# Turning a residual sum and an input into channels: VectorE's 32x32 blocks read back from DRAM in place of TensorE's transposes

## The chip, the core and the metric

The kernel runs on one NeuronCore of a Trainium2 chip. Its engines are TensorE (PE in the profile, its weight loads PEld), VectorE (DVE), ScalarE (ACT), GpSimd (POOL) and SyncE (SP). DMAs are issued by an engine's instruction stream: here by SP (queue q1) and by ACT (queue q10). The metric is the device time of one execution in microseconds (us); lower is better.

## The reference

One layer of a decoder trunk over 512 tokens of 2048 channels, in float32, and a final RMSNorm. The part that matters here is its end:

```python
x = x + einsum('btc,cd->btd', y_mix, w_out)          # 512x2048 @ 2048x2048: the residual sum, "x2" below
gate = sigmoid(einsum('btd,de->bte', x, w_pg) + b_pg)  # 512x2048 @ 2048x2048
x = x + gate * einsum('btq,qd->btd', p, w_ple)       # p is 512x256, w_ple 256x2048
return rms_norm(x, final_g)
```

Everything ahead of it (the input projections, a recurrence over 16 heads, a pooling group) produces `y_mix`.

## The kernel before, in words

**Tiles.** T = 512 tokens are NT = 4 tiles of P = 128; D = 2048 channels are KT = 16 steps of 128; an output block is EC = 512 channels, so that there are four, `ec` = 0 to 3. TensorE contracts over partitions, so a left operand has to lie channels by tokens. All large products are made of three float32r products of a high and a low part (`mm3`: hi·hi, hi·lo, lo·hi); `split` and `wsplit` make the two parts, the high one by a cast on ACT, the low one by a subtraction on DVE.

**The projections (`proj`).** For an output block, `proj` walks 16 weight steps. A step loads 256 KB of weights on SP (`raw_o`, `raw_g`: four buffers), splits it into `whi` and `wlo` (four buffers each; cast on ACT, subtraction on DVE) and issues 12 matmuls: 4 token tiles by 3 products. So a load may be issued only when DVE has made the low part of the step four back, and a cast only when TensorE has finished the step four back. A tile name such as `raw_g0_7` is the block (0) and the weight step (7).

**The out-projection** (`acc_o`, blocks 0 to 3) comes first. After each block DVE adds x (`x2_..`, line 1026) and ACT's queue stores the sum to DRAM as `x2d` (line 1027), 128 rows by 512 channels at a time. `turn` then makes channels out of tokens: 16 TensorE transposes of 128x128 into PSUM (`px2_..`, line 1033; the profile calls the tile `px`), and a `split` of each of the four 128x512 results into `x2hi` and `x2lo`, which are what the gate products (`acc_g`) contract. For blocks 0 to 2 `turn` runs while the next block's matmuls go on; for block 3 it is called from inside the first gate block, behind its third step (`aside`), and followed by the loads of the first embedding rows (`recall(0, lp)`, tiles `pler`). The gate block reads the channels of x2's block 3 only from its weight step 12 on.

**The gate stage.** Three blocks and then a last one with an order of its own. Each block reads its x2 rows again from DRAM (`fetch`, tiles `x2r`, line 1134), the embedding product (`pler`) and two rows of parameters (`bB`, `gB`), all on ACT's queue.

**The input p.** Before the out-projection, while the last head pair's recurrence runs, ACT's queue loads p (`pn`, line 927), TensorE transposes it (8 transposes, tile `ppt`, line 161) and two splits give `phi` and `plo` for the embedding product (`pple`). The recurrence has a chain of its own through SP: `xw` is written to DRAM (`xd`), read back as `x1` (tile `x` in the profile, line 689) and turned by DVE (`y1`, line 732) before TensorE's small products can start.

**The order.** Up to the out-projection TensorE's order is that of the program (`pin`). Behind it a scheduler places instructions on each engine; each engine then runs its own list in order and waits where it must. A DMA reports on one of eight completion semaphores in turn, shared by the two queues, and a DMA that is given one of them waits until that semaphore's previous DMA has landed.

Of the kernel before, what the change touches and what calls it, by code (L numbers as in the profile page):

```python
# [9 lines left out]
F32 = mybir.dt.float32  # L10
# [5 lines left out]
P = 128  # L16
T = 512
D = 2048
KT = D // P
NT = T // P  # L20
# [5 lines left out]
DPLE = 256  # L26
# [8 lines left out]
def trunk_kernel(ctx: ExitStack, tc: tile.TileContext, x, p, norm_g, w_in, mu, w0, w_up, a0, a_up,  # L35
                 k_k, k_a, r_k, ln_w, ln_b, w_pool, pool_scale, w_out, w_ple, w_pg, b_pg, final_g, out):
    nc = tc.nc
    PSUM = bass.MemoryType.PSUM
    x, p, w_in, w_out, w_ple, w_pg = x[0], p[0, 0], w_in[0], w_out[0], w_ple[0], w_pg[0]
    out = out[0]  # L40

    cst = ctx.enter_context(tc.tile_pool(name="cst", bufs=1))
    dram = ctx.enter_context(tc.tile_pool(name="dram", bufs=2, space=bass.MemoryType.DRAM))
# [4 lines left out]
    psM = s2.enter_context(tc.tile_pool(name="psM", bufs=3, space=PSUM))  # L48
# [45 lines left out]
    for h in range(2):  # L94
        rows = slice(64 * h, 64 * h + 64)
# [40 lines left out]
    def split(hi, lo, src):  # L136
        c_ = nc.scalar.copy(hi, src)
        nc.vector.tensor_tensor(lo, src, hi.bitcast(F32), ALU.subtract)
        return c_
# [20 lines left out]
    def tr(*a):  # L160
        i = nc.tensor.transpose(*a)
        return tc.keep_in_program_order(i) if pin[0] else i

    def mm3(ps, wh, wl, xh, xl, first, last):
        mm(ps, wh, xh, start=first, stop=False)
        mm(ps, wh, xl, start=False, stop=False)
        return mm(ps, wl, xh, start=False, stop=last)
# [293 lines left out]
    def stream():  # L461
        for kind, nm, j in jobs:
            if kind == "b":
                yield from pool_unit(j)
                continue
            if kind == "e":
                yield from embed_unit(j)
                continue
            if kind == "p":
                for k in range(2):  # L470
                    pt = psM.tile([P, T], F32, name=f"ppt{k}", tag="m")
                    for tt in range(NT):
                        tr(pt[:, tt * P:(tt + 1) * P], pn[0][:, tt, k * P:(k + 1) * P], ident)
                    a_ = rw.tile([P, T], F32R, name=f"phi{k}", tag=("sk", "sr")[k], bufs=2)
                    b_ = rw.tile([P, T], F32R, name=f"plo{k}", tag=("sv", "sg")[k], bufs=2)
                    split(a_, b_, pt)
                    phl.append((a_, b_))
                yield 3
                continue
            ps = psA.tile([P, T], F32, name=f"z{nm}{j}", tag="acc")  # L480
            yield from zcols(ps, f"{nm}{j}")
            t_ = rw.tile([P, T], F32, name=f"s{nm}{j}", tag=f"s{nm}", bufs=2)
            if nm == "g":
                silu2(ps, t_)
            else:
                shifted(ps, t_, {"r": 0, "k": 8, "v": 16}[nm] + j)
            zt[nm, j] = t_
# [429 lines left out]
    for j in range(NJ):  # L917
        def between():
            pump(H3 if j + 1 < NJ else HC[2])
            if j + 1 < NJ:  # L920
                scores(j + 1)
                pump_to(H2)

        if j + 1 == NJ:
            pn.append(rw.tile([P, NT, DPLE], F32, name="pn", tag="ar", bufs=2))
            for h in range(2):
                nc.scalar.dma_start(out=pn[0][:, 2 * h:2 * h + 2, :],
                                    in_=p[256 * h:256 * h + 256, :].rearrange("(t p) q -> p t q", p=P))
        if j + 1 < NJ:
            prepare(j + 1)  # L930
        elif gates:
            gates.pop()()
        recur(j, invert(j + 1) if j + 1 < NJ else iter(()), between)
        if j + 1 < NJ:
            gather(j + 1)
# [21 lines left out]

    x2hi = hp.tile([P, KT, T], F32R, name="x2hi", tag="ahi")
    x2lo = hp.tile([P, KT, T], F32R, name="x2lo", tag="alo")
    x2d = dram.tile([T, D], F32, name="x2d", bufs=1)  # L960

    KEEP, LATE = 8, 4
    TP = 40
# [4 lines left out]
        pool, tag = (psB, "accb") if nacc[0] % 5 in (1, 2, 3) else (psA, "acc")  # L968
        return pool.tile([P, EC], F32, name=nm, tag=tag)

    def proj(w, hi_, lo_, ec, nm, ks=range(KT), tts=range(NT), keep=None, aside=None):
        acc = {tt: acc_tile(f"acc_{nm}{ec}_{tt}") for tt in tts}
        for i, k in enumerate(ks):
            src = w[k * P:(k + 1) * P, ec * EC:(ec + 1) * EC].unsqueeze(1)
            if nm == "o" and ec == 0 and i + AHEAD < KT:
                load_y(ks[i + AHEAD])
            if (f"{nm}{ec}_{k}", 0) in ready:
                wh, wl = ready.pop((f"{nm}{ec}_{k}", 0))
            elif nm == "o" and ec == 0 and i < 4:
                wh, wl = chunk(f"{nm}{ec}_{k}", 0)  # L980
            elif keep is None or LATE <= i < KT - KEEP:
                wh, wl = wsplit(src, 1, EC, f"{nm}{ec}_{k}")
            else:
                raw = wp.tile([P, 1, EC], F32, name=f"raw_{nm}{ec}_{k}", tag="raw")
                nc.sync.dma_start(out=raw, in_=src)
                if i < 2:
                    if i == 0:
                        two = [pp.tile([P, 2, EC], F32R, name=f"{g}k", tag=g, bufs=1) for g in ("dh", "dl")]
                    wh, wl = (g[:, i:i + 1, :] for g in two)
                else:  # L990
                    own = i < KT - 4
                    wh, wl = ((kp_ if own else wp).tile([P, 1, EC], F32R, name=f"{g}k{k}",
                                                        tag=f"{g}k{k}" if own else g) for g in ("whi", "wlo"))
                split(wh, wl, raw)
                keep[k] = (wh, wl)
                if i >= LATE:
                    continue
            for tt in tts if keep is None or i >= LATE else tts[:-1]:
                ts_ = slice(tt * P, (tt + 1) * P)
                first = i == (LATE if keep is not None and tt == NT - 1 else 0)  # L1000
                e_ = mm3(acc[tt], hi_[:, k, ts_], lo_[:, k, ts_], wh[:, 0, :], wl[:, 0, :], first, i == KT - 1)
            if aside is not None and i == 2:
                with tc.issue_after(e_.ins):
                    hi = aside()
                with tc.issue_after(hi.ins):
                    recall(0, lp)
        return acc

    ples = {}
# [1 line left out]
    def recall(ec, pool):  # L1011
        ples[ec] = []
        for tt in range(NT):
            t_ = pool.tile([P, EC], F32, name=f"pler{ec}_{tt}", tag="ple", bufs=4)
            nc.scalar.dma_start(out=t_, in_=pled[tt * P:(tt + 1) * P, ec * EC:(ec + 1) * EC])
            ples[ec].append(t_)

    for ec in range(D // EC):
        es = slice(ec * EC, (ec + 1) * EC)
        acc = proj(w_out, yhi, ylo, ec, "o", order)  # L1020
        x2 = []
        for tt in range(NT):
            rows = slice(tt * P, (tt + 1) * P)
            t_ = pp.tile([P, EC], F32, name=f"x2_{ec}_{tt}", tag=("u", "sw")[tt // 2])
            nc.scalar.dma_start(out=t_, in_=x[rows, es])
            nc.vector.tensor_tensor(t_, acc[tt], t_, ALU.add)
            nc.scalar.dma_start(out=x2d[rows, es], in_=t_)
            x2.append(t_)
        def turn(ec=ec, x2=x2):
            for i in range(EC // P):  # L1030
                pt = psM.tile([P, T], F32, name=f"px2_{ec}_{i}", tag="m")
                for tt in range(NT):
                    nc.tensor.transpose(pt[:, tt * P:(tt + 1) * P], x2[tt][:, i * P:(i + 1) * P], ident)
                hi = split(x2hi[:, 4 * ec + i, :], x2lo[:, 4 * ec + i, :], pt)
            return hi


        if ec < D // EC - 1:
            turn()

    sy.close()


    with tc.tile_pool(name="fp", bufs=2) as fp, tc.tile_pool(name="kp_", bufs=1) as kp_:
        x3 = [fp.tile([P, D], F32, name=f"x3_{tt}", bufs=1) for tt in range(NT)]
        ssq = [fp.tile([P, D // EC + 1], F32, name=f"ssq{tt}", bufs=1) for tt in range(NT)]
        LAST = D // EC - 1
        WIDE, ENDS = 256, 6
# [82 lines left out]

        def fetch(ec, tt):
            x2_ = fp.tile([P, EC], F32, name=f"x2r{ec}_{tt}", tag="x2r", bufs=4)
            nc.scalar.dma_start(out=x2_, in_=x2d[tt * P:(tt + 1) * P, ec * EC:(ec + 1) * EC])
            pre[tt] = (x2_, ple[tt])

        for ec in range(LAST):
            pre = {}
            vec = vectors(ec)
            acc = proj(w_pg, x2hi, x2lo, ec, "g", aside=turn if ec == 0 else None)  # L1140
            ple = ples.pop(ec)
            recall(ec + 1, fp if ec % 2 == 0 else lp)
            for tt in range(NT):
                fetch(ec, tt)
                gate(acc[tt], ec, tt, slice(ec * EC, (ec + 1) * EC), ec)
# [66 lines left out]
```

## Time and profile before

| | |
|---|---|
| device time, median of 3 runs | 1085.23 us (1083.53 to 1088.02) |
| the profiled execution: its time, its span | 1082.7 us, 1081.0 us |
| mean granted TensorE clock | 0.998 |
| busy: PE, PEld, DVE, ACT, POOL | 1056.6, 872.1, 714.0, 441.5, 75.0 us |
| DMA queue q1 (SP): packets, MB | 192126, 112.28 |
| DMA queue q10 (ACT): packets, MB | 20704, 33.56 |

The span is the time from the first to the last instruction that was profiled; the execution's own time is 1.7 us more. A row of the profile names the line, the engine, the operation and the tiles (out<-in), then its count, its busy time and the mean duration of one in ns, and last the idle time of the engine just ahead of it with what ended it. Matmul durations overlap: the pitch from start to start is the price, not the duration.

### The profile page before, as it was taken

What the parts mean: (1) busy time and instruction counts of PE and PEld (TensorE: products, weight loads), DVE (VectorE), ACT (ScalarE), POOL (GpSimd) and SP (SyncE); (2) the same over time, 40 slices, a digit from 0 to 9 for tenths busy, and PEclk for the clock granted to TensorE, in tenths of its full rate; (3) what the DMA queues carried; (4) which work ended last, traced back from release to release, by engine and by line L of the source; (5) the groups of instructions that cost most, each with busy time, mean ns of one, the idle gap of its engine ahead of it and who ended that gap; (6) DMA issues with size and microseconds to landing.
All of it is one profiled execution on the core that took longest, in us unless ns stands there. A gap on an engine that the chain in (4) does not pass through costs nothing.

```text
span 1081.0 us, 17106 instructions
## 1 busy us (share of the span) xinstructions
PE 1056.6 (98%) x5996; PEld 872.1 (81%) x5996; DVE 714.0 (66%) x1851; ACT 441.5 (41%) x901; POOL 75.0 (7%) x180
## 2 busy tenths in 40 slices
PE   5999999999999999999999999999999999999996
PEld 4888878888888887878788788888888888888885
DVE  6676978888779789787887857563432424445356
ACT  7633435335335354353352344553222222333337
POOL 2100010110110100200101201000000000000000
PEclk9999999999999999999999999999999999999999
DMA  7434443342634533434435343774434428355434
GB/s 236 117 115 111 139 116 88 116 120 74 168 88 114 144 89 105 120 89 112 106 91 158 100 129 111 239 243 141 171 121 143 166 98 271 122 182 161 169 98 156
DMA packets 212916, 146.94 MB, mean 136 GB/s; under 512 B 68085, under 2 KB 173150, under 8 KB 212830
## 3 DMA queue, kind: packets, MB, share of 16 engines
q1 hardware_dynamic: 192126, 112.28, 35.9%
q10 hardware_dynamic: 20704, 33.56, 9.4%
q8 instruction: 47, 0.77, 0.3%
q14 instruction: 39, 0.32, 0.1%
HBM read 122.21 MB, written 23.07 MB: 134 GB/s over the span
## 4 chain that ended last, share of the span: by engine, by line
PE 91%; DVE 4%; DMA 3%; ACT 2%; issue 1%; ACTq 0%; SPq 0%; DVEq 0%
PE acc_o L157 16%; PE acc_g L157 16%; PE zb L157 14%; PE zv L157 8%; PE zg L157 8%; PE zr L157 8%; PE zk L157 7%; PE py L157 2%; PE pu L157 2%; PE pple L157 2%; PE pm L157 1%; DMA n<-nd 1%; PE pp L157 1%; PE ps L157 1%; DMA xt<-in_x_dram 1%; PE pmv L157 1%
## 5 line engine op out<-in xcount | busy, mean ns | idle before, releaser
L133 DVE TENSOR_TENSOR wlo_g<-raw_g,whi_g 128x512 fp32r<-128x512 f32 x84 | 57.0, 685 | 74.4 <-ACT whi_g L132 72.3
L157 PE MATMUL zb<-hhi,whi_b 128*128 128x512 f32 x256 | 106.0, 414 | 0.0
L133 DVE TENSOR_TENSOR wlo_o<-raw_o,whi_o 128x512 fp32r<-128x512 f32 x64 | 43.9, 690 | 90.9 <-ACT whi_o L132 90.8
L157 PE MATMUL zb<-hhi,wlo_b 128*128 128x512 f32 x256 | 100.4, 392 | 0.0
L157 PE MATMUL acc_o<-whi_o,ylo 128*128 128x512 f32 x256 | 100.2, 391 | 0.0
L157 PE MATMUL acc_o<-whi_o,yhi 128*128 128x512 f32 x256 | 99.9, 390 | 0.0
L157 PE MATMUL zb<-hlo,whi_b 128*128 128x512 f32 x256 | 99.8, 390 | 0.0
L157 PE MATMUL acc_o<-wlo_o,yhi 128*128 128x512 f32 x256 | 99.7, 389 | 0.0
L132 ACT CAST whi_g<-raw_g 128x512 fp32r<-128x512 f32 x84 | 52.0, 621 | 105.3 <-PE acc_g L157 58.9
L157 PE MATMUL acc_g<-whi_g,x2hi 128*128 128x512 f32 x208 | 81.2, 391 | 0.0
L832 POOL TENSOR_SCALAR s0p<-sbd,pw 64x64 f32<-64x64 f32 x96 | 58.0, 604 | 332.0 <-DVE sbd L825 243.5
L157 PE MATMUL acc_g<-wlo_g,x2hi 128*128 128x512 f32 x208 | 80.9, 389 | 0.0
L157 PE MATMUL acc_g<-whi_g,x2lo 128*128 128x512 f32 x208 | 80.6, 389 | 0.0
L132 ACT CAST whi_o<-raw_o 128x512 fp32r<-128x512 f32 x64 | 39.9, 623 | 96.3 <-PE acc_o L157 96.3
L132 ACT CAST whi_b<-raw_b 128x512 fp32r<-128x512 f32 x64 | 39.7, 621 | 86.7 <-PE zb L157 29.2
L133 DVE TENSOR_TENSOR wlo_b<-raw_b,whi_b 128x512 fp32r<-128x512 f32 x64 | 43.6, 683 | 27.3 <-ACT whi_b L132 27.1
L157 PEld LDWEIGHTS zb<-hhi,wlo_b 128*128 128x128 f32 x256 | 48.0, 188 | 10.9
L678 DVE TENSOR_TENSOR xw<-xw,tm 128x60 f32<-128x60 f32 (+24 forms) x248 | 52.1, 210 | 7.0
L157 PEld LDWEIGHTS acc_o<-wlo_o,yhi 128*128 128x128 f32 x256 | 48.1, 188 | 9.9
L157 PEld LDWEIGHTS acc_o<-whi_o,ylo 128*128 128x128 f32 x256 | 48.1, 188 | 9.8
L157 PEld LDWEIGHTS acc_o<-whi_o,yhi 128*128 128x128 f32 x256 | 48.1, 188 | 9.7
L157 PEld LDWEIGHTS zb<-hhi,whi_b 128*128 128x128 f32 x256 | 48.2, 188 | 8.3
(283 smaller groups left out, 2529.6 us busy)
## 6 DMA issues: line engine op xcount, KB each, us to landing
raw_b<-in_w_in_dram SPq DMA_DIRECT2D x64, 256.0 KB
raw_o<-in_w_out_dram SPq DMA_DIRECT2D x64, 256.0 KB
raw_g<-in_w_pg_dram SPq DMA_DIRECT2D x64, 256.0 KB
raw_k<-in_w_in_dram SPq DMA_DIRECT2D x32, 256.0 KB
raw_r<-in_w_in_dram SPq DMA_DIRECT2D x32, 256.0 KB
raw_v<-in_w_in_dram SPq DMA_DIRECT2D x32, 256.0 KB
raw_g<-in_w_in_dram SPq DMA_DIRECT2D x32, 256.0 KB
bkd<-bk SPq DMA_DIRECT2D x8, 512.0 KB
```

The source lines that it names most:

```text
L132: nc.scalar.copy(hi, raw)
L133: nc.vector.tensor_tensor(lo, raw, hi.bitcast(F32), ALU.subtract)
L157: i = nc.tensor.matmul(*a, **k)
L678: nc.vector.tensor_tensor(xw[:, 0:n_, s + 1:32], xw[:, 0:n_, s + 1:32], tm[:, 0:n_, 0:w_], ALU.add)
L832: nc.gpsimd.tensor_scalar(s0p[hc, :], nxt[hc, hc], pcn[hc], None, ALU.mult)
```

## The change

Three things move.

1. **x2's blocks.** `x2d` is now laid out in DRAM by block, by 128 channels, by token: `[4, 4, 512, 128]`. It is stored in pieces of 512 bytes (four for each token, where there was one of 2048 bytes) and read by `fetch` in such pieces. `turn` reads a block back from it with four SP DMAs, one for each group of 32 partitions, in pieces of 32 elements (128 bytes): partition 32q + k, piece (c, b) holds token 32b + k, channels 128c + 32q to + 31. DVE's transpose, which turns each 32x32 block in itself, then gives channels by tokens. The 64 TensorE transposes are gone; there are 16 DVE transposes of 128x512 from SBUF to SBUF, and the casts and subtractions of `split` read SBUF.
2. **The last block's place.** `aside` is gone. `turn` of block 3 is called ahead of the gate blocks and uses `x3_0` and `x3_1` (tiles of the final result, free until then) as its buffers; `recall(0, lp)` is called there too, and the scheduler places those loads in the out-projection's first block.
3. **p.** `pn` is loaded by eight SP DMAs in 128-byte pieces, in place of two on ACT's queue, and turned by two DVE transposes; 8 TensorE transposes are gone.

```diff
             if kind == "p":
                 for k in range(2):
-                    pt = psM.tile([P, T], F32, name=f"ppt{k}", tag="m")
-                    for tt in range(NT):
-                        tr(pt[:, tt * P:(tt + 1) * P], pn[0][:, tt, k * P:(k + 1) * P], ident)
+                    pt = rw.tile([P, T], F32, name=f"ppt{k}", tag=("kk", "kp")[k])
+                    nc.vector.transpose(pt.rearrange("p (b k) -> p b k", k=32), pn[0][:, k])
...
-            pn.append(rw.tile([P, NT, DPLE], F32, name="pn", tag="ar", bufs=2))
-            for h in range(2):
-                nc.scalar.dma_start(out=pn[0][:, 2 * h:2 * h + 2, :],
-                                    in_=p[256 * h:256 * h + 256, :].rearrange("(t p) q -> p t q", p=P))
+            pn.append(rw.tile([P, 2, T // 32, 32], F32, name="pn", tag="ar", bufs=2))
+            for q in range(4):
+                for c in range(2):
+                    nc.sync.dma_start(out=pn[0][32 * q:32 * q + 32, c],
+                                      in_=p[:, c * P + 32 * q:c * P + 32 * q + 32].rearrange("(b k) i -> k b i", k=32))
...
-    x2d = dram.tile([T, D], F32, name="x2d", bufs=1)
+    x2d = dram.tile([D // EC, EC // P, T, P], F32, name="x2d", bufs=1)
...
-            if aside is not None and i == 2:
-                with tc.issue_after(e_.ins):
-                    hi = aside()
-                with tc.issue_after(hi.ins):
-                    recall(0, lp)
...
-            nc.scalar.dma_start(out=x2d[rows, es], in_=t_)
+            nc.scalar.dma_start(out=x2d[ec, :, rows, :].rearrange("c t e -> t c e"),
+                                in_=t_.rearrange("p (c e) -> p c e", e=P))
...
-        def turn(ec=ec, x2=x2):
+        def turn(blocks, turned, ec=ec):
+            for q in range(4):
+                nc.sync.dma_start(out=blocks[32 * q:32 * q + 32].rearrange("p c b k -> p (c b) k"),
+                                  in_=x2d[ec].rearrange("c (b k) (q i) -> q k (c b) i", k=32, i=32)[q])
             for i in range(EC // P):
-                pt = psM.tile([P, T], F32, name=f"px2_{ec}_{i}", tag="m")
-                for tt in range(NT):
-                    nc.tensor.transpose(pt[:, tt * P:(tt + 1) * P], x2[tt][:, i * P:(i + 1) * P], ident)
-                hi = split(x2hi[:, 4 * ec + i, :], x2lo[:, 4 * ec + i, :], pt)
-            return hi
+                t_ = turned(i)
+                nc.vector.transpose(t_.rearrange("p (b k) -> p b k", k=32), blocks[:, i])
+                split(x2hi[:, 4 * ec + i, :], x2lo[:, 4 * ec + i, :], t_)
 
         if ec < D // EC - 1:
-            turn()
+            turn(ymp.tile([P, EC // P, T // 32, 32], F32, name=f"x2g{ec}", tag="x2g"),
+                 lambda i: ymp.tile([P, T], F32, name="x2t", tag="x2t"))
...
+        turn(x3[0].rearrange("p (c b k) -> p c b k", c=EC // P, k=32), lambda i: x3[1][:, i * T:(i + 1) * T])
+        recall(0, lp)
...
-            nc.scalar.dma_start(out=x2_, in_=x2d[tt * P:(tt + 1) * P, ec * EC:(ec + 1) * EC])
+            nc.scalar.dma_start(out=x2_.rearrange("p (c e) -> p c e", e=P),
+                                in_=x2d[ec, :, tt * P:(tt + 1) * P, :].rearrange("c t e -> t c e"))
...
-            acc = proj(w_pg, x2hi, x2lo, ec, "g", aside=turn if ec == 0 else None)
+            acc = proj(w_pg, x2hi, x2lo, ec, "g")
```

**Where it stands in the order.** On DVE, at the opening of the gate stage (`x2_3_3` is the last sum of block 3, `wlo_g0_7` the low part of gate step 7), the list before:

```order
L1026 TENSOR_TENSOR x2_3_3_9430<-acc_o3_3_9129,x2_3_3_9430 128x512
L133 TENSOR_TENSOR wlo_g0_3_9550<-raw_g0_3_9547,whi_g0_3_9549 128x512
L133 TENSOR_TENSOR wlo_g0_4_9568<-raw_g0_4_9565,whi_g0_4_9567 128x512
L133 TENSOR_TENSOR wlo_g0_5_9586<-raw_g0_5_9583,whi_g0_5_9585 128x512
L138 TENSOR_TENSOR x2lo_8100<-px2_3_0_9511,x2hi_8099 128x512
L138 TENSOR_TENSOR x2lo_8100<-px2_3_1_9518,x2hi_8099 128x512
L138 TENSOR_TENSOR x2lo_8100<-px2_3_2_9525,x2hi_8099 128x512
L138 TENSOR_TENSOR x2lo_8100<-px2_3_3_9532,x2hi_8099 128x512
L133 TENSOR_TENSOR wlo_g0_6_9604<-raw_g0_6_9601,whi_g0_6_9603 128x512
L133 TENSOR_TENSOR wlo_g0_7_9622<-raw_g0_7_9619,whi_g0_7_9621 128x512
```

and now (`x3_0` holds the block read back, `x3_1` what the DVE transposes make of it):

```order
L133 TENSOR_TENSOR wlo_g0_5_9553<-raw_g0_5_9550,whi_g0_5_9552 128x512
L133 TENSOR_TENSOR wlo_g0_6_9571<-raw_g0_6_9568,whi_g0_6_9570 128x512
L1032 STREAM_TRANSPOSE x3_1_9421<-x3_0_9420 128x512 x3
L138 TENSOR_TENSOR x2lo_8100<-x3_1_9421,x2hi_8099 128x512 x3
L1032 STREAM_TRANSPOSE x3_1_9421<-x3_0_9420 128x512
L133 TENSOR_TENSOR wlo_g0_7_9589<-raw_g0_7_9586,whi_g0_7_9588 128x512
L133 TENSOR_TENSOR wlo_g0_8_9607<-raw_g0_8_9604,whi_g0_8_9606 128x512
L138 TENSOR_TENSOR x2lo_8100<-x3_1_9421,x2hi_8099 128x512
```

All four transposes and three low parts of x2 now stand ahead of the weight part `wlo_g0_7`, and the first transpose waits for all four DMAs of the block.

On SP, at the same place, the gate weight loads stood in one row (`raw_g0_4` to `raw_g0_12`, nothing between). Now:

```order
L129 DMA raw_g0_4_9532<-in_w_pg_dram 128x512
L129 DMA raw_g0_5_9550<-in_w_pg_dram 128x512
L129 DMA raw_g0_6_9568<-in_w_pg_dram 128x512
L1028 DMA x3_0_9420<-x2d_8101 32x64x32 x4
L129 DMA raw_g0_7_9586<-in_w_pg_dram 128x512
L129 DMA raw_g0_8_9604<-in_w_pg_dram 128x512
```

The four reads stand ahead of the weights of step 7 in SP's list. The first of them waits for the four stores of block 3's sum; by the shared completion semaphores the second waits for `gB0`, the third for `pler1_3` and the fourth for `x2r0_0`, all three issued on ACT's queue.

On DVE in an earlier block (here while block 2 of the out-projection runs and block 1 of x2 is turned; the weight steps are taken in the order 8 to 13, 0 to 7, 14, 15, so `wlo_o2_2` is the ninth) the four subtractions stood right behind the sums and ahead of `wlo_o2_11`. Now:

```order
L133 TENSOR_TENSOR wlo_o2_0_8891<-raw_o2_0_8888,whi_o2_0_8890 128x512
L133 TENSOR_TENSOR wlo_o2_1_8909<-raw_o2_1_8906,whi_o2_1_8908 128x512
L1032 STREAM_TRANSPOSE x2t_8760<-x2g1_8755 128x512
L138 TENSOR_TENSOR x2lo_8100<-x2t_8760,x2hi_8099 128x512
L133 TENSOR_TENSOR wlo_o2_2_8927<-raw_o2_2_8924,whi_o2_2_8926 128x512
L1032 STREAM_TRANSPOSE x2t_8764<-x2g1_8755 128x512
L133 TENSOR_TENSOR wlo_o2_3_8945<-raw_o2_3_8942,whi_o2_3_8944 128x512
```

The first transpose stands behind the eighth weight step's low part and ahead of the ninth's. On SP the four reads (`x2g1`) stand behind the load of the eighth step, `raw_o2_1`, and ahead of the ninth's.

More of the change, by code (lines that the diff above doesn't have):

```diff
@@ L969, in acc_tile, with proj @@
         return pool.tile([P, EC], F32, name=nm, tag=tag)
-    def proj(w, hi_, lo_, ec, nm, ks=range(KT), tts=range(NT), keep=None, aside=None):
+    def proj(w, hi_, lo_, ec, nm, ks=range(KT), tts=range(NT), keep=None):
         acc = {tt: acc_tile(f"acc_{nm}{ec}_{tt}") for tt in tts}
@@ L1000, in proj @@
                 first = i == (LATE if keep is not None and tt == NT - 1 else 0)
-                e_ = mm3(acc[tt], hi_[:, k, ts_], lo_[:, k, ts_], wh[:, 0, :], wl[:, 0, :], first, i == KT - 1)
-            if aside is not None and i == 2:
-                with tc.issue_after(e_.ins):
-                    hi = aside()
-                with tc.issue_after(hi.ins):
-                    recall(0, lp)
+                mm3(acc[tt], hi_[:, k, ts_], lo_[:, k, ts_], wh[:, 0, :], wl[:, 0, :], first, i == KT - 1)
         return acc
```

## The prediction, made before the changed kernel ran

> **What bounds the kernel now.** I read the page first: busy times, then the chain that ended last.
>
> ```profile
> span 1081.0 us, 17106 instructions
> PE 1056.6 (98%) x5996; PEld 872.1 (81%) x5996; DVE 714.0 (66%) x1851; ACT 441.5 (41%) x901; POOL 75.0 (7%) x180
> PE 91%; DVE 4%; DMA 3%; ACT 2%; issue 1%; ACTq 0%; SPq 0%; DVEq 0%
> ```
>
> TensorE is busy for 98% of the span and carries 91% of the chain; DVE has a third of its time free. An instruction taken from TensorE should then shorten the run by its pitch, as long as nothing that feeds TensorE becomes late. So the second view is the chain from 715 us on, where the out-projection begins (start, length, what).
>
> ```profile
> 715.63 43.52 PE acc_o L157 x192
> 759.15 1.06 PE px L1033 x9
> ...
> 804.60 1.06 PE px L1033 x9
> ...
> 850.05 1.06 PE px L1033 x9
> ...
> 895.49 8.17 PE acc_g L157 x36
> 903.65 1.31 PE px L1033 x12
> 904.97 0.70 PE acc_g L157 x3
> 906.15 53.85 PE acc_g L157 x237
> ```
>
> The chain is TensorE's own work without a break, the transposes (`px`) among it. The first row gives the pitch of a matmul, 43.52 / 192 = 0.2267 us, and of a weight step of 12, 2.72 us.
>
> **Part 1: the transposes leave TensorE.** From one transposing group to the next (759.15, 804.60, 850.05) pass 45.45 us; 192 matmuls take 43.52 of them. A block of 16 transposes thus costs 1.93 us, three cost 5.8. In the gate stage, from 895.49 to 906.15 (10.66 us) stand 39 matmuls (8.84 us): 1.8 us for the fourth. For p:
>
> ```profile
> 650.78 1.04 PE L161 MATMUL ppt<-ident,pn 128*128 128x128 f32 x8
> 651.66 0.39 PE L157 MATMUL py<-sbd,ar 128*128 128x128 f32 x2
> ```
>
> 8 transposes, 651.66 - 650.78 = 0.9 us. Sum: 5.8 + 1.8 + 0.9 = 8.5 us off the path, 0.78% of 1085.
>
> The Trainium skill (VectorE: DVE Perf Modes, "Rules for kernel authors") speaks against this part: it gives a 128x128 transpose to TensorE where a PSUM destination will do, and blocks of 32x32 to DVE. Its table in "The three transpose paths" has 390 ns for one on TensorE (bf16); by that, an estimate, 72 would be 28 us to gain. The trace's rows have 0.12 us for one, and its number decides: there is much less to win here than the Trainium skill's price suggests.
>
> **Part 2: work given to DVE and ACT.**
>
> ```profile
> L617 DVE STREAM_TRANSPOSE bkn<-bg 128x512 f32<-128x512 f32 x16 | 10.9, 697 | 0.0
> L138 DVE TENSOR_TENSOR x2lo<-px,x2hi 128x512 fp32r<-128x512 f32 x16 | 10.3, 686 | 8.8 <-ACT x2hi L137 8.8
> L137 ACT CAST x2hi<-px 128x512 fp32r<-128x512 f32 x16 | 8.6, 593 | 15.7 <-PE px L1033 15.7
> L132 ACT CAST whi_g<-raw_g 128x512 fp32r<-128x512 f32 x84 | 52.0, 621 | 105.3 <-PE acc_g L157 58.9 <-PE zb L157 15.5 <-DMA raw_g<-in_w_pg_dram 11.4
> L133 DVE TENSOR_TENSOR wlo_g<-raw_g,whi_g 128x512 fp32r<-128x512 f32 x84 | 57.0, 685 | 74.4 <-ACT whi_g L132 72.3 <-DMA x2r<-x2d 2.1
> ```
>
> 18 transposes at 0.70 us are 12.5 us of DVE, of which 11.1 lie behind 715 us; a cast from SBUF costs 0.62 where one from PSUM cost 0.59. Both engines sit idle there most of the time (74 us ahead of `wlo_g` alone, waiting for casts that wait for TensorE), so I cost the work at nothing. What counts is its place: a transpose that waits for a DMA holds up the weight parts behind it.
>
> **Part 3: the transfers.** A block is stored in 512-byte pieces, and read back by four SP DMAs of 2048 pieces of 128 bytes, 8192 in all. The nearest thing in the trace is `bg`, four DMAs of 1024 such pieces:
>
> ```profile
> L662 SPq DMA_DIRECT2D bg<-bkd x32: 568/617/3007, 85.0 to 593.5; - x32
> DMA packets 4509, 1.12 MB, mean 187 GB/s; under 512 B 3075, under 2 KB 4508, under 8 KB 4508
> DMA packets 1198, 0.24 MB, mean 241 GB/s; under 512 B 962, under 2 KB 1198, under 8 KB 1198
> 905.00:917.00 12.00, 12.00 (x56) 9.80 (x55) 5.00 (x8) 4.18 (x8) 0.00 (x0) 1.00 1.03 371
> ```
>
> The second row is the stretch 590:596 us, the third 595:596, both with `bg` moving beside 512-byte packets; the last is the gate stage's opening, where the DMA engines are full (share 1.03) at 371 GB/s. At the best, 1198 packets in a us, a block's 8192 take 6.8 us; counting only the 962 small ones, 8.5; at the mean of the six us, gaps included (752 a us), 10.9. I take 8.5, the rate of small packets among others, and keep 6.8 to 10.9. An issue cost 0.6 us of SP for 1024 pieces; I take 1.2 for 2048, hidden by the transfer itself.
>
> The Trainium skill (DMA: Bandwidth & Descriptors, "Specifications") has 512 bytes as the least transfer at line rate, with a read-modify-write below. Its fit in "Anatomy of one DMA" (for the GpSimd path), 2.0 us and bytes over 436e3, would put a block's 1 MB at 4.4 us, an estimate from that page. The rows above agree with the first and not with the second: 0.24 MB in their best us.
>
> **Where the reads meet the path: blocks 0 to 2.** B is TensorE's start on the next block.
>
> ```profile
> 757.74 2.48 DVE L1026 TENSOR_TENSOR x<-acc_o,x 128x512 f32<-128x512 f32 x4
> 758.46 2.12 ACTq L1027 DMA_DIRECT2D x2d<-x  x4
> 763.88 0.34 ACTq L1025 DMA_DIRECT2D x<-in_x_dram  x1
> ```
>
> B is 758.99 here. The reload of x at 763.88 overwrites a stored tile, so the first store had landed within 5.4 us of its issue; I let the last one (512-byte pieces, issued by 760.6) land at B + 5.3. Then the reads go out, beside 1 MB of x (2.8 us at 371 GB/s). 5.3 + 8.5 + 2.8 and some latency: B + 17, between B + 15 and B + 20. Behind it DVE transposes (0.70), ACT casts (0.62), DVE subtracts (0.69) and only then makes the ninth weight step's low part (0.69): 2.7 us, so B + 19.7. TensorE wants that step at B + 8 x 2.72 = B + 21.8. The weights of that step, queued behind the reads on SP, land about when the reads do. 2.1 us to spare, no stall; at the late end 0.9 us in each of the three.
>
> **The last block.** G is TensorE's first gate matmul (895.32 us in the profiled execution).
>
> ```profile
> 894.79 2.12 ACTq L1027 DMA_DIRECT2D x2d<-x  x4
> 898.66 0.37 ACTq L1015 DMA_DIRECT2D pler<-pled  x1
> 901.04 2.30 ACTq L1015 DMA_DIRECT2D pler<-pled  x3
> 895.32 0.39 PE L157 MATMUL acc_g<-whi_g,x2hi 128*128 128x512 f32 x1
> ```
>
> The stores land at about G + 5, and reads 1 and 2 start. Read 3 waits for `pler1_3`, issued behind the cast of step 5 at some G + 7 (as the third of these rows) and sharing with the reads: 4.3 + 2.8 us of transfers from G + 5, so G + 12. Read 4 waits for `x2r0_0`, issued behind the cast of step 6 (TensorE is through step 2 at G + 8.2) and landed at G + 13. Reads 3 and 4 (4.3 us, with the rest of `x2r` beside them) end at G + 17.5; with the better price and no sharing G + 14.5, with the worse G + 20. Then in order: transpose 0.70, cast of x2 0.62, cast `whi_g0_7` 0.62 (its weights are queued behind read 4), two more casts of x2 1.2, the third subtraction 0.69, the fourth transpose 0.70, `wlo_g0_7` 0.69, with overlaps of back-to-back instructions (0.62 a piece, as in 2.48 for 4) 4.8 us: G + 22.3. TensorE is due at step 7 at G + 7 x 2.72 = G + 19.0, and its list has the four products with `whi_g0_7` first, 0.9 us. Stall 22.3 - 19.0 - 0.9 = 2.4; I take 2.5, with 0 and 5 as the ends. The channels themselves are wanted only at step 12, G + 32.6, and are there by G + 24. That `recall(0, lp)` now runs in the first out block costs nothing: DMA has room there, and it frees 1 MB in the gate stage's full stretch.
>
> **The recurrence.** SP's list now has p's eight DMAs around `xd` and `x1`. The third `x1` read, which DVE's second `y1` transpose waits for, moves behind a weight load that before stood ahead of it as its second:
>
> ```profile
> 627.30 0.39 SPq L129 DMA_DIRECT2D raw_b<-in_w_in_dram  x1
> 627.73 1.00 SPq L689 DMA_DIRECT2D x<-xd  x2
> 630.63 0.43 DVE L732 STREAM_TRANSPOSE y<-x 32x256 f32<-32x256 f32 x1 [0.53 <-DMA x<-xd]
> 633.64 0.28 PE L157 MATMUL pq<-y,mt 32*32 32x32 f32 x6
> ```
>
> It goes from 627.7 to about 628.8, and the second transpose from 630.6 to 632 or, behind `wlo_b12_1` which now stands ahead of it, 632.8, done at 633.2; TensorE takes it at 633.64. No stall, 0.5 us at the worst. The two DVE transposes of p fall among recurrence steps, with 10 us before TensorE needs `phi`: nothing.
>
> **The sum.** -8.5 + 2.5 = -6.0 us: 1082.7 - 6.0 = 1076.7 for the profiled execution. That execution is 2.5 us under the median of the runs (1085.23), so for a median I give 1079.2, in round figures 1079.
>
> **Rivals.**
> *Full gain.* The last block's reads are as quick as 6.8 us, or the waits for `pler1_3` and `x2r0_0` are short, so that they land by G + 15 and no stall is left: 1085.2 - 8.5 = 1076.7. For it: before, TensorE sat out the full DMA stretch 905 to 917 without idling. Against it: the reads add 8192 packets to that stretch. The Trainium skill's fit (DMA: Bandwidth & Descriptors, "Anatomy of one DMA"), 4.4 us a block by the estimate above, would lead here.
> *The gain is given back.* The reads take the late end, 10.9 us and the latency with it, so that three blocks stall 0.9 and the last one 5: 7.7 of 8.5 us, and 1084.4. For it: the gaps in the six-us row. Against it: those gaps belong in part to waits between `bg`'s four issues.
> *Slower.* The reads hold up weights in earnest. Each us over 8.5 is, beyond the 2.1 to spare, paid in three blocks and in the last in full: stall = 3(e - 2.1) + 2.5 + e. It eats the 8.5 us at e = 3.1 (11.6 us a block) and makes the run 0.5% slower at e = 4.5 (13). At 15 us a block, 22.2 us of stall: 1085.2 - 8.5 + 22.2 = 1099. For it: a `bg` issue that took 3.0 us (first row of part 3), so the queue can push back. Against it: no six us with such packets ran at under 752 a us.
>
> **Chances.** A change under 0.5% can hardly be told from none here: the three runs spread over 0.4%. That is 1079.8 and 1090.7. Forecast (one stall of 1 to 4 us in the last block, 1077.5 to 1081.5): 0.38, of which 0.25 lie under 1079.8. Full gain 0.22. Given back 0.27, all within 0.5%. Slower 0.13. So faster 0.47, same 0.40, slower 0.13. The range: from full gain less the scatter of the runs, 1075, through given back up into the slower case, 1088, which leaves some 0.2 outside, most of it above.
>
> **What the profile after would show.** No `px` or `ppt` on TensorE; the 192 matmuls of an out block in 43.5 us from block to block, or the missing part of a stall at the ninth step. The first transpose of the last block's `x3` at G + 17 to 18, `wlo_g` of step 7 at G + 22, and one idle stretch of TensorE of about 2.5 us there. `x2g` and `x3` reads of 8 to 9 us. The prediction is wrong if TensorE idles in all four blocks (the price of a 128-byte piece), if the last block shows no idle time, or if the recurrence shows a new wait for `y`.

## The result, and the profile after

| | before | after |
|---|---|---|
| device time, median of 6 runs each | 1085.61 us (1083.21 to 1088.02) | 1094.20 us (1089.26 to 1094.55) |
| ratio to before, 95% interval | | 1.0071 [1.0047, 1.0094] |
| the profiled execution: span, mean clock | 1081.0 us, 0.998 | 1092.8 us, 0.990 |

The change made the kernel 0.7% slower; 1079 was forecast. The two profiled executions differ by 11.8 us and the medians by 8.6, since the execution of before that was profiled was a quick one (1082.7). The page after has these lines for the first three that the prediction showed (span, busy times, chain), and the line of DMA packets:

```profile
span 1092.8 us, 17027 instructions
PE 1052.5 (96%) x5924; PEld 866.1 (79%) x5924; DVE 724.7 (66%) x1869; ACT 441.5 (40%) x901; POOL 74.3 (7%) x180
PE 83%; DVE 6%; DMA 6%; ACT 2%; SPq 2%; issue 1%; ACTq 0%; DVEq 0%
DMA packets 261908, 151.13 MB, mean 138 GB/s; under 512 B 105301, under 2 KB 226238, under 8 KB 261822
```

TensorE is busy for 4 us less and the span is 12 us longer. TensorE's share of the chain fell from 91% to 83%; DMA and SP's issues (SPq) rose from 3% and 0% to 6% and 2%. To find the place, cut the span at the first matmuls of the stages. Windows of after, TensorE only (length, busy, clock, DMA share, GB/s): the out-projection, the first gate block, the rest.

```profile
716.80:891.60 174.80, 174.61 (x769) 1.00 0.68 175
891.60:952.30 60.70, 47.48 (x193) 0.86 0.68 156
952.30:1083.60 131.30, 131.30 (x594) 1.00 0.49 155
```

The same cuts in the trace of before give 179.85, 45.37 and 131.27 us. So the out-projection gained 5.0 us, the first gate block lost 15.3, and nothing else moved; the out-projection began 1.3 us later, which the last experiment below shows to be scatter. The waits of TensorE behind 715 us:

```profile
PE acc_g L157 <- ACT whi_g L132: 12.2, 1, 12.2
PE acc_g L157 <- DVE wlo_g L133: 1.0, 1, 1.0
PE acc_o L157 <- DVE wlo_o L133: 0.2, 1, 0.2
```

One wait of 12.2 us and one of 1.0, both in the first gate block. An ideal block lasts 192 x 0.2267 = 43.5 us; 60.7 - 43.5 - 13.2 leaves 4.0 us that no wait explains. The clock does. Windows of after around the wait (TensorE idle from 910.8 to 923.1):

```profile
911.00:914.00 3.00, 0.00 (x0) 1.00 1.32 193
914.00:916.00 2.00, 0.00 (x0) 0.60 1.32 213
923.00:931.00 8.00, 6.95 (x16) 0.50 0.38 119
932.00:934.00 2.00, 2.00 (x11) 1.00 0.38 130
```

The granted clock fell to one half some 3.6 us into the idle time and came back only at 931.5, 8 us after work had begun again. What ended the 12.2 us stands in the chain of after (start, length, what):

```profile
773.17 6.65 DMA x2g<-x2d
...
779.91 0.72 DVE x2t L1032
...
781.91 0.70 DVE wlo_o L133
...
782.65 109.14 PE acc_o L157 x479
891.80 5.23 PE acc_g L157 x24
...
898.20 9.31 DMA pler<-pled
907.53 2.44 SPq L1028
...
910.01 1.60 SPq L1028
...
911.71 4.18 SPq L129
...
916.46 4.69 DMA raw_g<-in_w_pg_dram
921.15 1.90 DVE x L1032 x3
```

Read from below: the transposes of the last block began when the fourth read had landed. The chain names weights (`raw_g`) there, but in the trace read 4 reports its landing at 921.07, and the four loads of weights behind it report between 921.57 and 923.53, when the transposes had begun. Read 3 was issued behind the landing of `pler`, an ACT load that is wanted only at the end of the second gate block, and read 4 behind read 3. That `pler` load took 9.3 us to land. The weights of step 7 were issued behind the reads on SP (L129 behind L1028) and landed at 921.57. So TensorE would have waited until 922.2 even with the transposes out of the way (the landing and a cast of 0.62 us): the weights, behind the reads on SP, were themselves late by nearly the whole wait, and the transposes' place on DVE added under 1 us. The upper rows are block 0 of the out-projection, where the same chain (read, transpose, `wlo_o`) just fits.

SP's row of the four reads in after, and the second read alone, which could be issued only when `gB` had landed at 901.01:

```profile
897.82 13.79 SPq L1028 DMA_DIRECT2D x<-x2d  x4
901.02 2.89 SPq L1028 DMA_DIRECT2D x<-x2d  x1
```

### The profile page after: what moved, and what is told of

It reads as the page before. It is cut to its first block, busy times and chain, and to the rows that moved or that the text cites. A ratio compares the mean times of both kernels' runs of the same rounds, so it can differ in the third digit from the quotient of the medians.

```text
span 1092.8 us, 17027 instructions
## 1 busy us (share of the span) xinstructions
PE 1052.5 (96%) x5924; PEld 866.1 (79%) x5924; DVE 724.7 (66%) x1869; ACT 441.5 (40%) x901; POOL 74.3 (7%) x180
## 4 chain that ended last, share of the span: by engine, by line
PE 83%; DVE 6%; DMA 6%; ACT 2%; SPq 2%; issue 1%; ACTq 0%; DVEq 0%
PE acc_g L157 15%; PE zb L157 14%; PE acc_o L157 14%; PE zv L157 8%; PE zr L157 8%; PE zk L157 6%; PE zg L157 6%; PE pple L157 2%; PE py L157 2%; DMA n<-nd 2%; PE pu L157 2%; SPq L1028 1%; PE pp L157 1%; PE ps L157 1%; PE pm L157 1%
## 5 line engine op out<-in xcount | busy, mean ns | idle before, releaser
L157 PE MATMUL acc_g<-whi_g,x2hi 128*128 128x512 f32 x208 | 82.0, 397 | 12.2 <-ACT whi_g L132 12.2
L157 PEld LDWEIGHTS acc_g<-whi_g,x2hi 128*128 128x128 f32 x208 | 39.7, 192 | 21.2 <-ACT whi_g L132 12.7
```

The lines of the kernel that those rows point to most:

```text
L157: i = nc.tensor.matmul(*a, **k)
```

## The experiments

G is TensorE's first gate matmul (891.64 in after). "The first gate block" is the time from G to the first matmul of the second gate block; ideal is 43.5 us.

**1. The last block by TensorE again.** Blocks 0 to 2 and p stay as changed.

```diff
+        def turn_pe(ec=ec, x2=x2):
+            for i in range(EC // P):
+                pt = psM.tile([P, T], F32, name=f"px2_{ec}_{i}", tag="m")
+                for tt in range(NT):
+                    nc.tensor.transpose(pt[:, tt * P:(tt + 1) * P], x2[tt][:, i * P:(i + 1) * P], ident)
+                hi = split(x2hi[:, 4 * ec + i, :], x2lo[:, 4 * ec + i, :], pt)
+            return hi
...
-        turn(x3[0].rearrange("p (c b k) -> p c b k", c=EC // P, k=32), lambda i: x3[1][:, i * T:(i + 1) * T])
-        recall(0, lp)
...
-            acc = proj(w_pg, x2hi, x2lo, ec, "g")
+            acc = proj(w_pg, x2hi, x2lo, ec, "g", aside=turn_pe if ec == 0 else None)
```

> Blocks 0 to 2 and p by DVE's blocks as in the changed kernel; block 3 by TensorE's 16 transposes behind the third gate step, as before, with the first embedding rows loaded there again. Theory A (the whole loss is the stall in the first gate block and the slow clock behind it): what is left is the gain of three blocks and p, 5.8 + 0.9 = 6.7 us, so about 1079 beside 1085.5 before, and no idle TensorE in the first gate block. Rival B (128-byte reads or 512-byte stores also cost time in the out-projection, or the p change does in the recurrence): 1083 or more, with TensorE waiting or out blocks over 43.6 us there.

Measured: 1078.74 us against 1085.1, ratio 0.9939 [0.9926, 0.9953]: -6.4 us. The only wait of TensorE from 715 us to the end:

```profile
PE acc_o L157 <- DVE wlo_o L133: 0.2, 1, 0.2
```

Theory A: three blocks and p by VectorE bring what was forecast of them, and the whole loss sits in the last block.

**2. The last block's reads later.** Nothing but the place of `turn` for block 3:

```diff
+            acc = proj(w_pg, x2hi, x2lo, ec, "g", at={10: lambda: read(blk), 11: lambda: back(blk, tnd)} if ec == 0 else {})
```

where `read` issues the four reads and `back` the transposes and splits, ahead of the matmuls of that gate step.

> The changed kernel with block 3's four reads issued behind the tenth gate weight load and its DVE transposes behind the low part of gate step 10; the gate reads these channels only at step 12. Theory A (the reads stood ahead of weights that were wanted sooner: order): steps 7 to 10 get their weights in time, the stall falls from 13.2 us to at most 2, no half clock, and the time is 1085.5 - 8.5 + 0 to 2 = 1077 to 1079. Rival C (the DMA engines have too much to move in these 30 us whatever the order): the stall moves to step 11 or 12 and stays over 5 us, with a slow clock behind it: 1085 or more.

Measured: 1081.55 us, ratio 0.9961 [0.9945, 0.9976]: -3.6 us. One read kept its early place, since the scheduler had room for it; the other three went behind the weights of step 10.

```profile
PE acc_g L157 <- ACT whi_g L132: 1.0, 1, 1.0
PE acc_g L157 <- DVE wlo_g L133: 0.6, 2, 0.4
```

Order alone takes the waits from 13.2 to 1.6 us (the first gate block lasts 46.3 us) and keeps the clock at 1.0 there. The longest, 1.0 us, does sit at step 11 (G + 30.9), where rival C put it, but it is not over 5 us: theory A. The profiled execution has a span of 1077.1 us, but the six runs spread from 1078.3 to 1083.4 and their median misses the forecast by 2.6 us; whether the stall is longer in the others is not shown.

**3. The same bytes in big pieces.** For block 3 alone. Its channels then hold other values, so that only the time of this kernel says something.

```diff
-                nc.sync.dma_start(out=blocks[32 * q:32 * q + 32].rearrange("p c b k -> p (c b) k"),
-                                  in_=x2d[ec].rearrange("c (b k) (q i) -> q k (c b) i", k=32, i=32)[q])
+                nc.sync.dma_start(out=blocks[32 * q:32 * q + 32].rearrange("p c b k -> p (c b k)"),
+                                  in_=x2d[ec, q].rearrange("(p r) e -> p (r e)", p=32))
```

> The changed kernel, but block 3's four reads fetch the same number of bytes in 32 pieces of 8 KB each instead of 2048 of 128 bytes (so the channels of block 3 are other values); same issue place, same waits. Theory D (the price of 128-byte pieces on the DMA engines makes the weights behind them late): 1 MB takes about 2.8 us at 371 GB/s in place of 7 to 10, the stall falls from 13.2 to about 5 and the time by 6 to 9 us, to 1085 to 1088. Rival E (the waits of reads 2, 3 and 4 for gB, pler and x2r, and the order, make them late whatever the pieces): the stall stays over 10 us and the time over 1090.

Measured: 1090.09 us, ratio 1.0055 [1.0038, 1.0071]. TensorE's wait, and SP's row for the four reads:

```profile
PE acc_g L157 <- ACT whi_g L132: 8.9, 1, 8.9
896.77 11.59 SPq L1029 DMA_DIRECT2D x<-x2d  x4
```

With 128 pieces in place of 8192 the wait fell to 8.9 us only: 3.3 under that of after, and 1.3 under that of the changed kernel's second profile (experiment 8). The four reads still took SP 11.6 us to issue (13.8 in after), since the last of them left only when a `pler` load had landed, at 908.05. Neither theory's numbers are met exactly: the pieces are an eighth to a quarter of the wait; the waits on other loads, what these loads move at the same time, and the order are the rest.

**4 and 5. Idle matmuls in the gap.**

```diff
+            if nm == "g" and ec == 0 and i == 7:
+                fill = psM.tile([P, T], F32, name="fill", tag="m")
+                with tc.issue_after(e_.ins):
+                    for _ in range(FILL):
+                        d_ = nc.tensor.matmul(fill, hi_[:, 0, 0:P], hi_[:, 0, :], start=True, stop=True)
```

With FILL = 52:

> The changed kernel with 52 idle matmuls of 128x512 put on TensorE between gate steps 6 and 7, 52 x 0.227 = 11.8 us, in the 12.6 us in which it waits; their result is not used. Theory F (TensorE's clock was granted at half speed because TensorE had stood idle): the clock stays at 1.0, the 18 matmuls from 923 to 931.7 take 4 us in place of 8.6 less the 1.2 us wait, and the time falls by 3 to 4 us to about 1091. Rival G (the clock falls for another reason, or the half-speed stretch hid behind late weights anyway): no change, 1094, or slower by up to 3 if the idle matmuls end after the weights are there.

Measured: 1092.12 us, ratio 1.0061 [1.0046, 1.0076]. Windows of this kernel, all engines (PE, PEld, DVE, ACT, POOL, clock, DMA share, GB/s):

```profile
910.00:924.00 14.00, 14.00 (x64) 11.59 (x63) 3.25 (x6) 2.50 (x5) 0.00 (x0) 1.00 1.08 204
924.00:932.00 8.00, 7.30 (x32) 5.72 (x31) 5.48 (x9) 3.01 (x6) 0.00 (x0) 1.00 0.44 140
```

The clock stayed at 1.0 here, so its fall follows TensorE's own idleness. The time is that of the changed kernel run again (experiment 8, 1092.08): the idle matmuls ended 1.3 us after the cast of `whi_g0_7`, which eats part of the saving, and what is left is within the scatter. So a shorter fill, FILL = 36:

> The idle matmuls between gate steps 6 and 7 once more, 36 instead of 52: 8.2 us, so that they end before the weights of step 7 are there (52 ended 1.3 us after them). TensorE then stands idle for 2 to 4 us instead of 10 to 12. Theory F (the clock drops because of a long idle time, and the half-speed stretch costs 3.3 us): the clock stays at 1.0 behind the gap and the time is 3 us below the changed kernel's, 1089 to 1090. Rival G: the same as the changed kernel, 1092 to 1094, or half clock in spite of the short gap.

Measured: 1091.60 us, ratio 1.0065 [1.0044, 1.0085]. Windows, TensorE only; the idle matmuls end at 920.1:

```profile
919.00:920.00 1.00, 1.00 (x5) 1.00 1.19 170
920.00:922.00 2.00, 0.07 (x1) 1.00 1.04 341
922.00:924.00 2.00, 0.47 (x1) 0.57 0.32 118
924.00:931.00 7.00, 6.03 (x14) 0.50 0.38 123
```

Theory F falls in the form in which it was put: a wait of 3.5 us is enough. The clock fell about 2.2 us into it and the work at half speed behind it lasted 9.0 us, against 8.4 behind the 12.2 us of after. The first gate block lasted 60.35 us here: 43.5, 8.2 of fill, 4.5 of waits, and 4.1 for the clock.

**6. The other loads later.** The reads and transposes stay where the change put them. ACT's loads of `pler1`, `x2r0` and the second `bB`, `gB` go behind the cast of gate step 12:

```diff
-            recall(ec + 1, fp if ec % 2 == 0 else lp)
+            with (tc.issue_after(cast["g0_12"].ins) if ec == 0 else ExitStack()):
+                recall(ec + 1, fp if ec % 2 == 0 else lp)
...
-                fetch(ec, tt)
+                with (tc.issue_after(cast["g0_12"].ins) if ec == 0 else ExitStack()):
+                    fetch(ec, tt)
```

> The changed kernel; block 3's reads and transposes stay where they are, but the loads on ACT's queue that the first gate block does not want until its end (four pler1, four x2r0, the second bB and gB; 2.6 MB) are issued behind the cast of gate step 12. Theory H (the reads are late because these loads share their stretch of the DMA engines and hold the completion semaphores that reads 2 to 4 wait for): the reads go out at G + 6 without waiting, end by G + 16 to 18, step 7 is ready at about G + 21 to 23, the stall falls from 13.2 to 2 to 4 us and its half clock to at most 1: 1085.2 - 8.5 + 2 to 5 = 1079 to 1082. Rival I (the pieces and the queue alone: four reads of 2048 pieces cannot be issued and moved in less than 20 us): the stall stays over 8 us, 1088 or more.

Measured: 1079.63 us, ratio 0.9942 [0.9925, 0.9958]: -6.0 us. The four reads on SP, the first transposes, and a window of all engines:

```profile
897.60 6.41 SPq L1030 DMA_DIRECT2D x<-x2d  x4
908.74 1.90 DVE L1034 STREAM_TRANSPOSE x<-x 128x512 f32<-128x512 f32 x3 [7.43 <-DMA x<-x2d]
898.00:908.00 10.00, 10.00 (x46) 8.29 (x45) 1.29 (x2) 0.62 (x1) 0.00 (x0) 1.00 1.27 148
```

The reads are issued in 6.4 us instead of 13.8 and are in SBUF by 908.74, G + 17.2. TensorE waits once, 1.9 us. Theory H, and within its numbers (the wait a little under its 2 to 4 us); rival I is out. The edit takes away two things at once, the waits on semaphores that these loads hold and what they move beside the reads; which of the two costs more is not shown.

**7. Both.** Experiments 2 and 6 in one kernel.

> The edits of the late reads and of the later ACT loads together: reads 2 to 4 behind the weights of gate step 10, transposes behind its low part, pler1, x2r0, bB and gB behind the casts of steps 12 to 15. Theory A and H together: no idle TensorE in the first gate block, the whole 8.5 us: 1076 to 1077.5, under both kernels and at least 1.5 us under the one with TensorE's transposes for block 3. Rival: x2r0 or pler1 now come late for the first gate block's end, or a lane wait moves to the weights, and 2 us or more are given back: 1079 or more.

Measured: 1077.35 us, ratio 0.9921 [0.9904, 0.9938]: -8.2 us, the fastest of all, under both kernels. The three stages, TensorE only:

```profile
716.00:890.00 174.00, 174.00 (x769) 1.00 0.65 176
890.00:933.50 43.50, 43.50 (x193) 1.00 0.85 213
933.50:1064.90 131.40, 131.40 (x594) 1.00 0.48 154
```

TensorE is busy without a gap from 716 us to its end, at full clock. The forecast's gain of 8.5 us was there to be had.

**8. The changed kernel again.**

> The changed kernel itself once more, in the same call as its variants: 1094 within 1.5 us, a ratio of 1.006 to 1.009, a stall of 12 to 14 us in the first gate block, half clock behind it. If the stall was an accident of one execution: under 1088.

Measured: 1092.08 us, ratio 1.0061 [1.0043, 1.0078], the waits 10.2 and 1.0 us, and the clock at half speed behind them. The wait differs by 2 us between the two profiles, but it is there in both.

**9 and 10. p alone, and before once more.**

```diff
-                        tr(pt[:, tt * P:(tt + 1) * P], pn[0][:, tt, k * P:(k + 1) * P], ident)
+                    nc.vector.transpose(pt.rearrange("p (b k) -> p b k", k=32), pn[0][:, k])
```

with p's loads as changed, and all of x2 as before.

> The kernel before with only p's part of the change: eight SP DMAs in 128-byte pieces and two DVE transposes in place of two loads on ACT's queue and eight TensorE transposes. By the prediction -0.9 us, 1084.5, which can't be told from no change. Rival J (p's reads hold up xd and x1 on SP, since the out-projection began 0.5 to 3 us later in the profiles of all changed kernels than in that of before): 1 to 3 us slower, 1086.5 to 1088.5, with TensorE waiting for y or sbd behind 618 us.

> The kernel before, for a second profile: the out-projection's first matmul at 715.5 us in the first. If rival J holds, it starts at 715.5 within 0.5 again, and at 717 or later with p's part; if that difference is the scatter of single executions, it starts anywhere from 715 to 718.

Measured: 1084.65 us, ratio 0.9998 [0.9986, 1.0011], and 1084.55 us for the one run of before. TensorE waits for nothing between 610 and 716 us in either. Two products that stand on both sides of p's transposes, first in the kernel with p's part, then in before:

```profile
621.47 1.15 PE L157 MATMUL py<-uv,mt 128*64 128x64 f32 x32
651.97 0.38 PE L157 MATMUL py<-sbd,ar 128*128 128x128 f32 x2
```

```profile
621.81 1.15 PE L157 MATMUL py<-uv,mt 128*64 128x64 f32 x32
653.18 0.39 PE L157 MATMUL py<-sbd,ar 128*128 128x128 f32 x2
```

30.50 us against 31.37: the 0.9 us are there in the trace, and too few for the median. The out-projection began at 715.76 and at 716.99, so its later start in after (716.80 against 715.47) is the scatter of single executions, and rival J is out.

## Why the prediction was wrong

- **The gain of 8.5 us: right.** Experiment 7 gives -8.2 in the median, and stage by stage 179.85 - 174.08 = 5.8 us in the out-projection, 45.37 - 43.52 = 1.9 in the first gate block, 0.9 for p: the three terms as forecast.
- **DVE and ACT for nothing: right.** Transposes measured 0.71 us, and no wait of TensorE goes back to their number, only to their place.
- **8192 pieces of 128 bytes at 8.5 us: right for the pieces, with too little at both ends.** With ACT's loads out of the way (experiment 6) the reads' packets ran from 898.91 to 907.22, 8.3 us (the window 898.9 to 907.23):

```profile
DMA packets 8364, 1.24 MB, mean 149 GB/s; under 512 B 8269, under 2 KB 8269, under 8 KB 8364
```

  From the first issue to the first transpose passed 908.74 - 897.60 = 11.1 us: 1.3 ahead of the first packet and 1.5 behind the last, where the forecast had "some latency". An issue on SP, put at 1.2 us, took 1.6 to 2.9 us for reads 2 to 4 of after. The Trainium skill's fit (DMA: Bandwidth & Descriptors, "Anatomy of one DMA"), which by the estimate in the prediction would give 4.4 us, is not borne out; its 512 bytes as the least transfer at line rate ("Specifications") agrees with the 149 GB/s of this row, against 371 in the prediction's row of the gate stage's opening.
- **Blocks 0 to 2, no stall: right, by a hair.** The first transposes started at B + 19.6, 19.3 and 18.9 us against a forecast of 17 (15 to 20), and the ninth step's low part was ready at B + 22.3 in block 0. The margin of 2.1 us was spent, and so was the one product of that step that needs no low part (0.23 us): 0.2 us of wait. The reads' packets took 10.6, 9.0 and 10.0 us there, beside the loads of x. The two out blocks beside which x2's blocks 0 and 1 were turned lasted 44.0 and 43.8 us where 43.5 is ideal: 0.8 us in all, the difference between the 5.0 us gained and the 5.8 forecast.
- **The last block, a stall of 2.5 us (0 to 5): this is the step that failed.** The reads were to end at G + 17.5; read 4 landed at G + 29.4 and the transposes began at G + 29.5. The forecast let reads 1 and 2 start at G + 5; read 1 left at G + 6.2 and read 2 waited for `gB` until G + 9.4. `pler1_3`, which read 3 waits for, was to land at G + 12; it took until G + 15.9. The prediction had given two reads and `pler`'s megabyte 4.3 + 2.8 us, each at the rate that it has alone (371 GB/s for the megabyte). Read 4 was to go out at G + 13, left at G + 18.4 behind read 3's issue, and took 11.1 us to land. The prediction had the 371 GB/s from 905 to 917 us of before. From 897 to 921 us of after the DMA engines were just as full and moved 198 GB/s:

```profile
897.00:921.00 24.00, 13.84 (x62) 11.12 (x60) 2.20 (x4) 1.26 (x3) 0.00 (x0) 0.86 1.09 198
```

  Two errors add up. The forecast left loads out: `x2r`, a megabyte like `pler`, got 0.2 us in it (read 4 at G + 13 and 4.3 us make G + 17.3; it says 17.5), and the second `bB` and `gB` got nothing. In these 24 us 4.76 MB moved, 1.05 of them the reads; by the forecast's own prices that is 8.5 us for the pieces and 10.0 for 3.7 MB at 371 GB/s, 18.5 us together, an estimate. And side by side, with reads that waited for loads, it took 24. Where the loads are away, the forecast's own timetable comes out: reads in at G + 17.2, a stall of 1.9 us (experiment 6).
- **What was not in the sum at all: the clock.** Half speed followed every wait of 3.5 us or more in this block and cost 3.4 to 4.2 us beyond the waits. In after it made 13.2 us of waits cost 17.2.
- **The rival "slower" named the wrong mechanism.** It let the price of a piece decide, in all four blocks; at 10.6 us at most in blocks 0 to 2, 2.1 over 8.5, that price stayed under its break-even of 3.1. What decided was a chain of waits in one block: an early load on the other queue, a shared completion semaphore, SP's list in order, and weights at its end.
- **recall(0) earlier costs nothing: true of itself,** but the room that it left in the gate's opening was taken by `pler1`, which now came at G + 4.
- **The recurrence: right.** No wait from 610 to 716 us.

## What to carry to other kernels

When an edit adds transfers to a stretch where the DMA engines are already full, add up all that is queued there on every queue, and ask of each transfer when it is wanted: here 2.6 MB that could wait over 20 us stood ahead of reads that could not, and moving them was worth more than the edit. On a queue whose instructions go in order, a transfer that waits holds up everything behind it; put it behind what is wanted first. And count a stall of TensorE of several us with another 3.4 to 4.2 us on top: that is what the clock cost behind waits of 3.5 us and more here.

## What the runs showed of the hardware

**The clock changes in steps of 3.41 us.** By the clock's records in the traces, half speed lasted 17.07 us in after, 13.65 us in experiments 3 and 8 and 10.24 us in experiment 5: 5, 4, 4 and 3 times 3.41 us. The rows below are TensorE in such steps: four of after, counted from the fall at 914.40; the step ahead of the fall in experiment 5; and a step of experiment 6, counted from its first change of clock, that holds nearly all of the 1.9 us wait.

```profile
910.99:914.40 3.41, 0.00 (x0) 1.00 1.30 202
924.64:928.05 3.41, 2.44 (x7) 0.50 0.20 55
928.05:931.47 3.42, 3.42 (x10) 0.50 0.76 246
931.47:934.88 3.41, 3.41 (x17) 1.00 0.24 82
918.86:922.28 3.42, 1.21 (x6) 1.00 1.08 287
911.92:915.34 3.42, 1.62 (x7) 1.00 0.13 33
```

The clock fell behind a step with no work or with 1.21 us of it, and stayed whole behind one with 1.62 us. It came back behind the first step in which TensorE worked throughout; the second wait, of 1.0 us, cost after one more step at half speed. So the fall came 2.2 to 3.9 us into the waits of 3.5, 8.9, 10.2 and 12.2 us, and waits of 1.0 us (experiment 2) and 1.9 us (experiment 6) left the clock at 1.0. A short wait is not always safe: between 485 and 493 us every trace has a wait of 1.1 us among small products, and in four of the twelve (experiments 2, 4, 5 and 8) one step at half speed followed it. The Trainium skill (TensorE: Matmul & The Clock Gate, "What's actually happening") has half speed after an idle window of about 3.4 us, and full speed after about as long a busy one. The traces agree on the length and on the way back, but the fall did not need a wholly idle step.

**SP's issue was held up behind the reads.** One weight load of 256 KB, which costs 0.33 to 0.39 us to issue elsewhere, took 4.18 us behind the four reads (the chain of after, 911.71). That a full queue is the reason is not shown.
